# Modulation sums in pairs behind chosen VectorE operations, an earlier one-row Fourier split, and seven raw weight slots

## The chip, the core and the metric

The kernel runs on one core of a Trainium2 chip. The metric is the device time of one execution in microseconds (us). Three executions of the kernel before were timed, and one more was profiled. Its engines are named as the profile names them: PE (TensorE; PEld is its weight load), DVE (VectorE), ACT (ScalarE), POOL (GpSimd) and SP (SyncE, which here only issues DMAs).

## What is computed

One layer of a diffusion backbone over 1024 latent tokens of width 1024 and 256 context tokens. What matters here is the first part, from the modulation to the output projection; the expert part is 16 experts of a SwiGLU network over 128 tokens each.

```
mod = silu(c) @ w_mod + b_mod
sh1, sc1, g1, sh2, sc2, g2 = split(mod, 6)
hx = rmsnorm(x) * (1 + sc1) + sh1          # and the context with its own rows
u_f, u_x, u_g = split(hx @ w_in)           # 512 columns each
y_f = fft2(u_f, 4 groups of 128).real
xc  = conv4(u_x)                           # 4 channel tiles of 128 in the kernel
r, i = sigmoid(xc @ wa + ba), sigmoid(xc @ wi + bi)     # two directions
a   = exp(-8 r softplus(-lam));  h_t = a h_(t-1) + sqrt(1 - a^2) (i xc)
y_r = (h_forward + h_backward) * gelu(u_g)
x   = x + g1 * (concat(y_f, y_r) @ w_out)
hx2 = rmsnorm(x) * (1 + sc2) + sh2
out = rmsnorm(x + g2 * experts(hx2))
```

## The kernel before

All products are made of three matmuls with fp32r operands: `split` (lines 226 to 232) writes a tensor's upper part on ACT (line 227) and the rest on DVE (line 228, `raw - hi`), and `mm3` (line 608) issues hi by hi, hi by rest and rest by hi (line 611). So no product can end before DVE has made the rest of its weights: these tiles are called `wl` for the input projection, `gl` for the gates, `wol` for the output projection, `xcl` for the convolved tokens, `abl` and the one-row `xl` for the Fourier part.

The part before the experts runs in three stages. `phase_a` loads, normalizes and projects the first two channel tiles. `phase_c` goes through the four channel tiles t of the recurrent group: `conv(t)` (line 649), `lru_front(t)` with the gate products `g` and the sigmoids, exponentials and square roots on ACT, `lru_back(t)` (line 808) with `lru_scan` (line 711: two products and one scan of 1280 elements for each direction) on DVE, and `gelu(t)` for its gate; in between it makes the Fourier projections `uf` (`fourier_a`, line 876) and sends results to DRAM. `phase_f` makes the rest of the Fourier part group by group (`fb_dft`, `fb_split`, `fb_trig` with the products `pq`, `fb_evac` with the tiles `T` and `yf`), splits the output weights and makes the output projection `mx`, 8 token tiles long. After it come the router and the experts.

Four rows of the modulation (g1, sc2, sh2, g2) are not made on PE: `mod_acc(r, h)` (line 826) sums eight 128x512 pieces of w_mod, each times a column of `cond`, on DVE into an accumulator `macc`. The pieces come two by two, 512 KB a load, into two `mraw` slots, from POOL's DMA queue; the finished accumulator goes to DRAM (`accd`). There are 8 such calls, so 64 DVE instructions in 32 pairs. `mod_row` (line 842) reads the accumulators back in `phase_f` and adds the bias row on DVE (line 850).

The order of the instructions on each engine is made by a scheduler from the written order, priorities and when it holds an instruction ready; `high_priority` raises instructions, `pin` keeps one in the written order. In the kernel before, the calls of `mod_acc` stand in `phase_c` from line 741 on, without `pin`. Raw weights go through 3 slots of 128x512 (`wraw`), loaded from SP's queue; the next load into a slot is issued once the slot's split is done.

Of the kernel before, what the change touches and what calls it, by code (L numbers as in the profile page):

```python
# [9 lines left out]
F32 = mybir.dt.float32  # L10
F32R = mybir.dt.float32r
# [3 lines left out]
ALU = mybir.AluOpType  # L15

D = 1024
N = 1024
NCTX = 256
# [142 lines left out]
class Kern:  # L162
# [72 lines left out]
    def prologue(self, stop=None):  # L235
        tc, nc, a = self.tc, self.nc, self.a
        self.lg = self.cst.tile([128, 8, E], F32, name="lg")
        self.NC4, self.NP1 = 19, 4
        self.pr = self.sr.enter_context(tc.tile_pool(name="pr", bufs=1, side="right"))
        self.pro = self.sl.enter_context(tc.tile_pool(name="pro", bufs=1, side="left"))  # L240
        for tag, n, w, dt in (("wraw", 3, 512, F32), ("mraw", 2, 1024, F32), ("whi", 5, 512, F32R),
                              ("wlo", 5, 512, F32R)):
            self.pro.tile([128, w], dt, tag=tag, name=f"z_{tag}", bufs=n)
        for tag in ("xc", "xs"):
            self.c5(f"z_{tag}", tag=tag)
        self.c4("z_c4")
# [37 lines left out]
    def phase_a(self):  # L284
# [12 lines left out]

        def prefetch(ct, h, ht=False):
            t = self.pr.tile([128, 4, 128], F32, tag="ht", name=f"wr{ct}_{h}", bufs=2) if ht else self.pro.tile(
                [128, 4, 128], F32, tag="wraw", name=f"wr{ct}_{h}", bufs=3)  # L300
            nc.sync.dma_start(t.rearrange("p k c -> p (k c)"), a["win"][ct, h])
            self.wraw[ct, h] = t

# [345 lines left out]
    def conv(self, t):  # L649
        nc = self.nc  # L650
        u = self.u.pop(t)
        xc = self.c5(f"xc{t}", tag="xc")
        col = lambda i: self.cols[:, COL["cw"] + 4 * i + t:COL["cw"] + 4 * i + t + 1]
        cb = self.cols[:, COL["cb"] + t:COL["cb"] + t + 1]
        for o, n, q in ((0, N, NCTX), (N, NCTX, 0)):
            nc.scalar.activation(xc[:, q:q + n], u[:, o:o + n], AF.Identity, scale=col(1), bias=cb)
            for i, a, b in ((0, 1, n), (2, 0, n - 1), (3, 0, n - 2)):
                nc.vector.scalar_tensor_tensor(xc[:, q + a:q + b], u[:, o + a + i - 1:o + b + i - 1], col(i),
                                               xc[:, q + a:q + b], op0=ALU.mult, op1=ALU.add)
        self.xc[t] = xc  # L660

    def xsplit(self, t):
# [2 lines left out]
        self.xs[t] = h, l  # L665

    def load_gate(self, t):
        w = self.pro.tile([128, 4, 128], F32, tag="wraw", name=f"gr{t}", bufs=3)
        self.nc.sync.dma_start(w.rearrange("p k c -> p (k c)"), self.a["wgate"][t])
        self.graw[t] = w  # L670

# [38 lines left out]

    def lru_scan(self, d, r, g, a):
        V = self.nc.vector
        V.scalar_tensor_tensor(r, a, 1.0, r, op0=ALU.add, op1=ALU.mult)
        V.tensor_tensor(r, r, g, op=ALU.mult)  # L714
        s = slice(None) if d == 0 else slice(None, None, -1)
        V.tensor_tensor_scan(g[:, s], a[:, s], r[:, s], 0.0, op0=ALU.mult, op1=ALU.add)  # L716

    def phase_c(self, stop=None):
        nc = self.nc
        self.xc, self.xs, self.graw, self.gw = {}, {}, {}, {}  # L720
        self.ysp = self.dram.tile([7, 128, N], F32, name="ysp")
        self.yl = {}
        self.accd = self.dram.tile([4, 2, 128, 512], F32, name="accd")
        st = {}
        self.load_gate(0)
        self.conv(0)
        self.xsplit(0)
        self.load_trig()
        self.ux(2)
        self.gate_w(0)  # L730
        self.get(7)
        st[0] = self.lru_front(0)
        self.load_gate(1)
        self.conv(1)
        self.xsplit(1)
        self.ux(3)
        self.get(0)
        self.gate_w(1)
        self.lru_back(0, *st[0])
        self.fourier_a(0)  # L740
        self.mod_acc(0, 0)
        self.conv(2)
        self.get(8)
        self.load_gate(2)
        st[1] = self.lru_front(1)
        self.mod_acc(0, 1)
        self.xsplit(2)
        self.gelu(0)
        self.mod_acc(1, 0)
# [5 lines left out]
        self.mod_acc(1, 1)  # L755
        self.get(9)
        self.load_gate(3)
        st[2] = self.lru_front(2)
        self.mod_acc(2, 0)
        self.xsplit(3)  # L760
        self.gelu(1)
        self.mod_acc(2, 1)
        self.gate_w(3)
        self.get(2)
        self.lru_back(2, *st[2])
        self.fourier_a(2)
        self.mod_acc(3, 0)
        self.get(3)
        st[3] = self.lru_front(3)
        self.fourier_a(3)  # L770
        self.get(10)
        self.lru_back(3, *st[3])
        self.gelu(2)
        self.get(11)
        self.fd = {}
        self.fb_dft(0)
        self.fb_split(0)
        self.gelu(3)
        self.mod_acc(3, 1)
# [28 lines left out]
    def lru_back(self, t, st, a):  # L808
        nc = self.nc
        for d in range(2):  # L810
            self.lru_scan(d, *st[d], a[d])
        g0, g1 = st[0][1], st[1][1]
        nc.vector.tensor_tensor(g0[:, NCTX:], g0[:, NCTX:], g1[:, 0:N], op=ALU.add)
        self.yl[t] = g0[:, NCTX:]

    def gelu(self, t):
# [5 lines left out]
        nc.vector.tensor_tensor(gg, gg, self.yl.pop(t), op=ALU.mult)  # L822
        self.dump(f"yr{t}", gg)
        nc.sync.dma_start(self.ysp[3 + t], gg)

    def mod_acc(self, r, h):
        nc, a = self.nc, self.a
        m, s = (2, 4, 3, 5)[r], slice(512 * h, 512 * h + 512)
        acc = self.pr.tile([128, 512], F32, tag="ht", name=f"macc{m}{h}", bufs=2)
        for kp in range(KD // 2):  # L830
            w = self.pro.tile([128, 2, 512], F32, tag="mraw", name=f"mraw{m}{h}{kp}", bufs=2)
            nc.gpsimd.dma_start(w, a["wmod"][m, 2 * kp:2 * kp + 2, :, s].rearrange("k p c -> p k c"))
            for i in range(2):
                k = 2 * kp + i
                c = self.cond[:, k:k + 1]
                if k == 0:
                    nc.vector.tensor_scalar(acc, w[:, i], c, None, op0=ALU.mult)
                else:
                    nc.vector.scalar_tensor_tensor(acc, w[:, i], c, acc, op0=ALU.mult, op1=ALU.add)  # L839
        nc.gpsimd.dma_start(self.accd[r, h], acc)  # L840

    def mod_row(self, r, acc, b, ones, p):
        nc = self.nc
# [32 lines left out]
    def fourier_a(self, g):  # L876
# [8 lines left out]
        V.tensor_tensor(U[:, 0, 1:], p[:, 1:512], rev, op=ALU.add)  # L885
        V.tensor_tensor(U[:, 1, 1:], p[:, 1:512], rev, op=ALU.subtract)
# [19 lines left out]
    def fb_split(self, g):  # L906
# [68 lines left out]
    def phase_f(self):  # L975
# [7 lines left out]
        raws = {}  # L983

        def wo_raw(k, h, tag):
            raw = self.pro.tile([128, 512], F32, tag=tag, name=f"wor{k}{h}", bufs=3 if tag == "wraw" else 5)
            nc.sync.dma_start(raw, a["wout"][k][:, 512 * h:512 * h + 512])
            raws[k, h] = raw

# [28 lines left out]

        def half(n, p=128):
            tag = "wraw" if "s2" in n and n != "brows21" and "sh2" not in n else "wlo"  # L1020
            return self.pro.tile([p, 512], F32, tag=tag, name=n, bufs=3 if tag == "wraw" else 5)

        def row(r, name):
            p = self.p3(f"rowp{name}")
# [804 lines left out]
```

## Time and profile before

| | |
|---|---|
| timed executions | 1966.42, 1969.73, 1971.72 us; median 1969.73 |
| profiled execution, its own time | 1968.55 us |
| span of the profiled execution | 1966.7 us |
| PE busy | 1883.7 us, 96% of the span |
| DVE busy | 1749.7 us, 89% |
| ACT busy | 1357.4 us, 69% |
| mean granted TensorE clock | 0.985 |

The span runs from the first to the last instruction; the profiled execution's own time is 1.85 us longer and 1.2 us under the median of the three. An engine's busy time adds up over stages with different limits, so the table alone doesn't say which engine ends what; the rows further down are taken stage by stage.

### The profile page before, as it was taken

Reading aid. Unit: us, or ns where it says so; the run is one execution under the profiler, and the core shown is the slowest. Engines: PE = TensorE matmul, PEld = TensorE weight load, DVE = VectorE, ACT = ScalarE, POOL = GpSimd, SP = SyncE. Lnnn points to the kernel's source line nnn. Section 1 sums busy time; section 2 is a strip of 40 time slices with the busy share of each in tenths; the row PEclk is TensorE's granted clock in tenths of the full one; section 3 lists DMA queues with packets and bytes.
Section 4 is the critical chain, followed back from the end, with each engine's and each line's share of the span. In section 5 each row is a group of like instructions: output and inputs, shape, how many; then the busy total and the mean of one; then the engine's idle time right before and its main releaser. Section 6 shows DMA issues by size and latency. Waiting matters only on the chain.

```text
span 1966.7 us, 23514 instructions
## 1 busy us (share of the span) xinstructions
PE 1883.7 (96%) x8944; PEld 1530.9 (78%) x8944; DVE 1749.7 (89%) x1626; ACT 1357.4 (69%) x1094; POOL 126.6 (6%) x126
## 2 busy tenths in 40 slices
PE   7989879969999999999999999999999999999996
PEld 2777767857788888888888888888888888888884
DVE  7889787789999989899999999998989898989987
ACT  6568643346677777777777777777777777777775
POOL 2311100220000000000000000000000000000000
PEclk9999989979999999999999999999999999999998
DMA  8443554578999999999999999999999999999994
GB/s 333 126 148 123 193 174 150 200 279 332 352 352 388 383 376 390 370 395 371 391 362 395 359 409 370 387 364 397 372 384 380 391 379 373 390 383 390 371 391 172
DMA packets 113952, 651.27 MB, mean 331 GB/s; under 512 B 12743, under 2 KB 20472, under 8 KB 46254
## 3 DMA queue, kind: packets, MB, share of 16 engines
q1 hardware_dynamic: 100718, 602.55, 79.6%
q0 software_dynamic: 10816, 38.82, 7.0%
q10 hardware_dynamic: 2304, 8.39, 1.1%
q8 instruction: 70, 1.15, 0.2%
q14 instruction: 44, 0.36, 0.0%
HBM read 622.98 MB, written 26.74 MB: 330 GB/s over the span
## 4 chain that ended last, share of the span: by engine, by line
PE 79%; DVE 8%; DMA 6%; issue 5%; ACT 1%; POOL 0%; SPq 0%; POOLq 0%; DVEq 0%; ACTq 0%
PE gu L611 46%; PE y L611 23%; PE mx L611 4%; DMA mraw<-in_wmod_dram 3%; DVE lo L228 3%; PE ht L1620 2%; DMA wm<-in_wmod_dram 1%; DVE macc L839 1%; PE xt L1492 1%; DMA trr<-in_trig_dram 1%; PE hp L1185 1%; PE pq L611 1%; ACT hi L227 1%; DVE g L716 0%; DVE r L714 0%
## 5 line engine op out<-in xcount | busy, mean ns | idle before, releaser
L228 DVE TENSOR_TENSOR lo<-raw,hi 128x2048 fp32r<-128x2048 f32 x525 | 1196.9, 2295 | 120.6 <-ACT hi L227 119.7
L227 ACT ACTIVATE hi<-raw 128x2048 fp32r<-128x2048 f32 x525 | 1007.0, 1918 | 303.2 <-PE gu L611 204.4
L611 PE MATMUL gu<-hi,xgh 128*128 128x512 f32 x1408 | 556.2, 395 | 0.0
L611 PE MATMUL gu<-lo,xgh 128*128 128x512 f32 x1408 | 548.7, 390 | 1.4 <-DVE lo L228 1.4
L611 PE MATMUL gu<-hi,xgl 128*128 128x512 f32 x1408 | 548.9, 390 | 0.0
L611 PEld LDWEIGHTS gu<-hi,xgl 128*128 128x128 f32 x1408 | 264.4, 188 | 56.4 <-DVE xgl L228 0.2
L611 PEld LDWEIGHTS gu<-lo,xgh 128*128 128x128 f32 x1408 | 264.8, 188 | 55.7 <-DVE lo L228 1.8
L611 PEld LDWEIGHTS gu<-hi,xgh 128*128 128x128 f32 x1408 | 264.6, 188 | 52.7 <-issue 0.2
L611 PE MATMUL y<-hi,hh 128*128 128x512 f32 x704 | 282.0, 401 | 0.0
L611 PE MATMUL y<-hi,hl 128*128 128x512 f32 x704 | 275.9, 392 | 1.3 <-DVE hl L228 1.3
L611 PE MATMUL y<-lo,hh 128*128 128x512 f32 x704 | 274.8, 390 | 0.0
L611 PEld LDWEIGHTS y<-hi,hl 128*128 128x128 f32 x704 | 132.4, 188 | 30.4 <-DVE hl L228 1.8
L611 PEld LDWEIGHTS y<-lo,hh 128*128 128x128 f32 x704 | 132.9, 189 | 25.9 <-issue 0.2
L611 PEld LDWEIGHTS y<-hi,hh 128*128 128x128 f32 x704 | 132.7, 189 | 25.3 <-issue 0.2
L1613 ACT ACTIVATE hid<-gu 128x512 f32<-128x512 f32 x96 | 54.0, 563 | 82.4 <-PE gu L611 82.4
L1630 POOL DMA_INDIRECT accx<-ys,idx x15 | 23.9, 1590 | 1002.8 <-DVE ys L1629 929.7
L228 DVE TENSOR_TENSOR hl<-ht,hh 128x512 fp32r<-128x512 f32 x96 | 61.3, 638 | 0.0
L1614 DVE TENSOR_TENSOR hid<-hid,gu 128x512 f32<-128x512 f32 x96 | 61.0, 635 | 0.0
L839 DVE SCALAR_TENSOR_TENSOR macc<-mraw,cond,macc 128x512 f32<-128x512 f32 x56 | 41.8, 747 | 20.4 <-DMA mraw<-in_wmod_dram 19.5
L1620 PE MATMUL ht<-k_ident,hid 128*128 128x128 f32 x352 | 54.2, 272 | 3.0 <-DVE hid L1614 3.0
L1620 PEld LDWEIGHTS ht<-k_ident,hid 128*128 128x128 f32 x352 | 43.8, 140 | 16.5 <-DVE hid L1614 4.5
L227 ACT ACTIVATE hh<-ht 128x512 fp32r<-128x512 f32 x96 | 52.0, 541 | 1.5 <-PE ht L1620 1.5
(430 smaller groups left out, 1791.4 us busy)
## 6 DMA issues: line engine op xcount, KB each, us to landing
raw<-in_wg_dram SPq DMA_DIRECT2D x160, 1024.0 KB, 7.1
raw<-in_wu_dram SPq DMA_DIRECT2D x160, 1024.0 KB, 7.5
raw<-in_wd_dram SPq DMA_DIRECT2D x160, 1024.0 KB, 7.6
raw<-in_wt_dram SPq DMA_DIRECT2D x32, 1024.0 KB, 7.8
mraw<-in_wmod_dram POOLq DMA_DIRECT2D x32, 512.0 KB, 4.7
raw<-in_wdt_dram SPq DMA_DIRECT2D x16, 1024.0 KB, 6.9
wm<-in_wmod_dram SPq DMA_DIRECT2D x16, 512.0 KB, 9.8
wr<-in_win_dram SPq DMA_DIRECT2D x24, 256.0 KB, 3.6
```

What stands on the lines that cost most here:

```text
L227: i = self.nc.scalar.activation(hi, src, AF.Copy)
L228: j = (eng or self.nc.vector).tensor_tensor(lo, src, hi, op=ALU.subtract)
L611: i = nc.tensor.matmul(out, l, r, start=st, stop=sp)
L839: nc.vector.scalar_tensor_tensor(acc, w[:, i], c, acc, op0=ALU.mult, op1=ALU.add)
L1185: self.pin(nc.tensor.matmul(q[:, 1024:1024 + E], hT[:, k], wr[:, k], start=k == 0, stop=k == KD - 1))
L1492: nc.tensor.transpose(p[:, 128 * i:128 * i + 128], xg[:, 128 * k:128 * k + 128], self.ident)
L1613: nc.scalar.activation(hid[:, 0:w], p[:, 0, 0:w], AF.Silu)
L1614: nc.vector.tensor_tensor(hid[:, 0:w], hid[:, 0:w], up, op=ALU.mult)
L1620: self.nc.tensor.transpose(q[:, c:c + 128], hid[:, c:c + 128], self.ident)
L1630: self.nc.gpsimd.indirect_dma_start(out=self.accx, out_offset=bass.IndirectOffsetOnAxis(ap=idx[:, :1], axis=0), in_=ys, in_offset=None, co ...
```

## The change

`mod_acc` becomes a generator, `mod_gen`, which yields after each pair of DVE instructions and issues the load of the next pair ahead of the pair it works on. Its loads, sums and stores are all pinned to the written order. A counter, `tick`, moves it on: chosen DVE instructions (the convolution, the two products and the scan of `lru_scan`, the sum of the two directions, the gate product, the Fourier sums) report a cost, and each time the reported costs pass 1.7 one pair is emitted behind the instruction. The counter is switched on just ahead of `lru_back(0)`; what is left of the 32 pairs is emitted after `gelu(3)`. In `fb_split` the one-row split comes ahead of the two large ones and is raised twice. The raw weight slots go from 3 to 7, and the memory for them comes from the scratch of the dynamic DMAs, 8192 bytes instead of the default.

```
-        for tag, n, w, dt in (("wraw", 3, 512, F32), ("mraw", 2, 1024, F32), ("whi", 5, 512, F32R),
+        for tag, n, w, dt in (("wraw", 7, 512, F32), ("mraw", 2, 1024, F32), ("whi", 5, 512, F32R),
...
-        V.scalar_tensor_tensor(r, a, 1.0, r, op0=ALU.add, op1=ALU.mult)
-        V.tensor_tensor(r, r, g, op=ALU.mult)
+        self.tick(V.scalar_tensor_tensor(r, a, 1.0, r, op0=ALU.add, op1=ALU.mult), 1.5)
+        self.tick(V.tensor_tensor(r, r, g, op=ALU.mult), 1.5)
         s = slice(None) if d == 0 else slice(None, None, -1)
-        V.tensor_tensor_scan(g[:, s], a[:, s], r[:, s], 0.0, op0=ALU.mult, op1=ALU.add)
+        self.tick(V.tensor_tensor_scan(g[:, s], a[:, s], r[:, s], 0.0, op0=ALU.mult, op1=ALU.add), 2.8)
...
+        self.mg, self.cost = self.mod_gen(), None
...
+        self.cost = 0.0
         self.lru_back(0, *st[0])
         self.fourier_a(0)
-        self.mod_acc(0, 0)
...
         self.gelu(3)
-        self.mod_acc(3, 1)
+        for _ in self.mg:
+            pass
...
+    STEP = 1.7
+
+    def tick(self, i, cost):
+        if self.cost is None:
+            return
+        self.cost += cost
+        while self.cost >= self.STEP:
+            self.cost -= self.STEP
+            next(self.mg, None)
+
+    def mod_gen(self):
...
+        load(0)
+        for n, (r, h, kp) in enumerate(todo):
+            load(n + 1)
...
+                    self.pin(nc.vector.scalar_tensor_tensor(acc, w[n][:, i], c, acc, op0=ALU.mult, op1=ALU.add))
...
+            yield
...
         with self.tc.high_priority(offset=self.HP):
+            with self.tc.high_priority(offset=self.HP):
+                self.split(px[0:1, 0:128], xh, xl)
             for s in range(2):
...
-            self.split(px[0:1, 0:128], xh, xl)
...
-    nc = _bacc.Bacc("TRN2", target_bir_lowering=False, num_devices=1)
+    nc = _bacc.Bacc("TRN2", target_bir_lowering=False, num_devices=1, dynamic_dma_scratch_size=8192)
```

Three places show what this makes of DVE's order. The number behind a tile's name is the buffer's; a scan is printed as SCALAR_TENSOR_TENSOR, too (line 716 before, 717 now).

The first place is DVE ahead of the first scans, where `xcl1` splits the second channel tile and `g01` is a gate product of the first; `macc` is the accumulator of the sums and `r00` the first operand of `lru_back(0)`. Before:

```order
L839 SCALAR_TENSOR_TENSOR macc21_1294<-mraw213_1307,cond_185,macc21_1294 128x512 x2
L837 TENSOR_SCALAR macc40_1369<-mraw400_1370,cond_185 128x512
L839 SCALAR_TENSOR_TENSOR macc40_1369<-mraw400_1370,cond_185,macc40_1369 128x512
L228 TENSOR_TENSOR xcl1_1034<-xc1_1024,xch1_1033 128x1280
L699 TENSOR_TENSOR g01_1009<-g01_1009,xc0_822 128x1024
L700 TENSOR_TENSOR g01_1009<-g01_1009,xc0_822 128x256
L839 SCALAR_TENSOR_TENSOR macc40_1369<-mraw401_1374,cond_185,macc40_1369 128x512 x2
L839 SCALAR_TENSOR_TENSOR macc40_1369<-mraw402_1378,cond_185,macc40_1369 128x512 x2
L839 SCALAR_TENSOR_TENSOR macc40_1369<-mraw403_1382,cond_185,macc40_1369 128x512 x2
L837 TENSOR_SCALAR macc41_1475<-mraw410_1476,cond_185 128x512
L839 SCALAR_TENSOR_TENSOR macc41_1475<-mraw410_1476,cond_185,macc41_1475 128x512
L713 SCALAR_TENSOR_TENSOR r00_983<-a00_1014,r00_983 128x1280
```

And now:

```order
L228 TENSOR_TENSOR wl0_1_1124<-wr0_1_1117,wh0_1_1123 128x512
L698 TENSOR_TENSOR g00_984<-g00_984,xc0_822 128x1280
L228 TENSOR_TENSOR xcl1_1034<-xc1_1024,xch1_1033 128x1280
L700 TENSOR_TENSOR g01_1009<-g01_1009,xc0_822 128x1024
L701 TENSOR_TENSOR g01_1009<-g01_1009,xc0_822 128x256
L714 SCALAR_TENSOR_TENSOR r00_983<-a00_1014,r00_983 128x1280
```

In all, 26 of the 64 sums stood ahead of `r00` on DVE, and none does now.

The second place is DVE in `lru_back(0)`; `wl8_0` and `wl8_1` are the rests of the weights that PE's next projection `ug` reads. Before:

```order
L714 TENSOR_TENSOR r00_983<-r00_983,g00_984 128x1280
L714 TENSOR_TENSOR r01_1008<-r01_1008,g01_1009 128x1280
L716 SCALAR_TENSOR_TENSOR g00_984<-a00_1014,r00_983 128x1280
L716 SCALAR_TENSOR_TENSOR g01_1009<-a01_1017,r01_1008 128x1280
L228 TENSOR_TENSOR wl8_0_1226<-wr8_0_1221,wh8_0_1225 128x512
L813 TENSOR_TENSOR g00_984<-g00_984,g01_1009 128x1024
L228 TENSOR_TENSOR wl8_1_1230<-wr8_1_1223,wh8_1_1229 128x512
```

And now:

```order
L717 SCALAR_TENSOR_TENSOR g00_984<-a00_1014,r00_983 128x1280
L856 SCALAR_TENSOR_TENSOR macc00_1137<-mraw200_1133,cond_185,macc00_1137 128x512
L715 TENSOR_TENSOR r01_1008<-r01_1008,g01_1009 128x1280
L856 SCALAR_TENSOR_TENSOR macc00_1137<-mraw201_1135,cond_185,macc00_1137 128x512
L717 SCALAR_TENSOR_TENSOR g01_1009<-a01_1017,r01_1008 128x1280
L856 SCALAR_TENSOR_TENSOR macc00_1137<-mraw201_1135,cond_185,macc00_1137 128x512
L810 TENSOR_TENSOR g00_984<-g00_984,g01_1009 128x1024
L856 SCALAR_TENSOR_TENSOR macc00_1137<-mraw202_1141,cond_185,macc00_1137 128x512
L228 TENSOR_TENSOR wl8_0_1259<-wr8_0_1254,wh8_0_1258 128x512
L856 SCALAR_TENSOR_TENSOR macc00_1137<-mraw202_1141,cond_185,macc00_1137 128x512
L228 TENSOR_TENSOR wl8_1_1263<-wr8_1_1256,wh8_1_1262 128x512
L856 SCALAR_TENSOR_TENSOR macc00_1137<-mraw203_1145,cond_185,macc00_1137 128x512
```

The sums of the pairs `mraw200` to `mraw203` now stand one by one between the scans and the splits.

The third place is DVE where the second Fourier group is split; `abl1` and `xl1` are its large and one-row splits, `T20` the evacuation of the first group's `pq0`, and `accg11` and `accs21` are bias additions of `mod_row`. Before:

```order
L813 TENSOR_TENSOR g30_1789<-g30_1789,g31_1814 128x1024
L228 TENSOR_TENSOR abl1_2134<-ab1_2089,abh1_2133 128x512
L822 TENSOR_TENSOR gg3_2037<-gg3_2037,g30_1789 128x1024
L947 TENSOR_TENSOR T20_2144<-pq0_2106,T10_2143 128x256
L948 TENSOR_TENSOR T20_2144<-pq0_2106,T10_2143 128x256
L949 TENSOR_TENSOR T20_2144<-pq0_2106,T10_2143 128x256
L228 TENSOR_TENSOR xl1_2136<-abx1_2098,xh1_2135 1x128
L950 TENSOR_TENSOR T20_2144<-T10_2143,pq0_2106 128x256
```

And now:

```order
L228 TENSOR_TENSOR wol6_2189<-wor61_2083,woh6_2188 128x512
L870 TENSOR_TENSOR accg11_2455<-accg11_2455,browg11_2457 1x512
L870 TENSOR_TENSOR accs21_2500<-accs21_2500,brows21_2502 1x512
L819 TENSOR_TENSOR gg3_2055<-gg3_2055,g30_1807 128x1024
L228 TENSOR_TENSOR xl1_2136<-abx1_2098,xh1_2135 1x128
L228 TENSOR_TENSOR abl1_2134<-ab1_2089,abh1_2133 128x512 x2
L968 TENSOR_TENSOR T20_2144<-pq0_2106,T10_2143 128x256
L969 TENSOR_TENSOR T20_2144<-pq0_2106,T10_2143 128x256
```

`xl1` has gone ahead of `abl1` and of the first `T20` rows, and two `wol6` splits and four bias additions, which stood behind these, now stand ahead of them.

## Rows read from the trace of the kernel before

**Rows 1.** The page's chain that ended last, share of the span by engine.

```profile
PE 79%; DVE 8%; DMA 6%; issue 5%; ACT 1%; POOL 0%; SPq 0%; POOLq 0%; DVEq 0%; ACTq 0%
```

**Rows 2.** Stretches: us, then each engine's busy us (instructions), TensorE clock, DMA.

```profile
core 0: us, PE busy (x) PEld busy (x) DVE busy (x) ACT busy (x) POOL busy (x), PEclk, DMA share, GB/s
85.60:134.30 48.70, 48.37 (x239) 40.27 (x239) 38.09 (x48) 28.60 (x32) 10.21 (x15) 1.00 0.59 177
128.70:268.80 140.10, 116.33 (x537) 93.93 (x535) 122.31 (x144) 90.39 (x92) 15.56 (x23) 0.95 0.46 149
...
268.90:282.00 13.10, 12.27 (x71) 11.14 (x71) 10.13 (x27) 3.79 (x9) 0.00 (x0) 0.76 0.68 231
282.00:400.00 118.00, 117.66 (x629) 95.11 (x628) 91.33 (x263) 42.83 (x77) 17.81 (x10) 1.00 0.49 172
```

**Rows 3.** What PE waited for from 134.3 to 283: us, times, longest.

```profile
PE ug L611 <- DVE wl L228: 8.6, 2, 6.8
PE abx L903 <- DVE xl L228: 6.4, 1, 6.4
PE uf L611 <- DVE wl L228: 5.4, 1, 5.4
```

**Rows 4.** DVE's sums from 80 to 130: busy, mean ns, idle before, its releaser.

```profile
L839 DVE SCALAR_TENSOR_TENSOR macc<-mraw,cond,macc 128x512 f32<-128x512 f32 x22 | 16.5, 751 | 7.2 <-DMA mraw<-in_wmod_dram 6.7
L837 DVE TENSOR_SCALAR macc<-mraw,cond 128x512 f32<-128x512 f32 x4 | 2.5, 622 | 3.4 <-DMA mraw<-in_wmod_dram 3.4
```

**Rows 5.** Timeline of ACT: start, us, instruction, the square roots of the first tile.

```profile
123.17 2.44 ACT L805 ACTIVATE r<-r 128x1280 f32<-128x1280 f32 x2
```

**Rows 6.** Timeline of DVE: start, us, instruction.

```profile
128.70 2.89 DVE L713 SCALAR_TENSOR_TENSOR r<-a,r 128x1280 f32<-128x1280 f32 x2
...
168.13 0.49 DVE L837 TENSOR_SCALAR macc<-mraw,cond 128x512 f32<-128x512 f32 x1
...
182.49 1.21 DVE L813 TENSOR_TENSOR g<-g,g 128x1024 f32<-128x1024 f32 x1
...
185.75 0.74 DVE L839 SCALAR_TENSOR_TENSOR macc<-mraw,cond,macc 128x512 f32<-128x512 f32 x1
186.41 0.68 DVE L228 TENSOR_TENSOR gl<-gr,gh 128x512 fp32r<-128x512 f32 x1
187.01 0.74 DVE L839 SCALAR_TENSOR_TENSOR macc<-mraw,cond,macc 128x512 f32<-128x512 f32 x1
...
268.62 0.14 DVE L952 TENSOR_TENSOR yf<-pq,T 128x1 f32<-128x1 f32 x1
...
272.83 1.27 DVE L850 TENSOR_TENSOR accg<-accg,browg 1x512 f32<-1x512 f32 x2
```

**Rows 7.** What DVE waited for from 128.7 to 268.8: us, times, longest.

```profile
DVE macc L839 <- DMA mraw<-in_wmod_dram: 12.8, 6, 4.2
DVE macc L837 <- DMA mraw<-in_wmod_dram: 2.4, 2, 1.3
```

**Rows 8.** Loads of the sums: the page's issue row (us to landing), DVE and POOL timelines.

```profile
mraw<-in_wmod_dram POOLq DMA_DIRECT2D x32, 512.0 KB, 4.7
...
81.02 0.75 DVE L839 SCALAR_TENSOR_TENSOR macc<-mraw,cond,macc 128x512 f32<-128x512 f32 x1
...
82.08 0.70 POOL L832 DMA_DIRECT2D mraw<-in_wmod_dram  x1 [7.06 <-DVE macc L839]
...
196.32 1.41 POOL L832 DMA_DIRECT2D mraw<-in_wmod_dram  x2
...
201.87 1.54 DVE L839 SCALAR_TENSOR_TENSOR macc<-mraw,cond,macc 128x512 f32<-128x512 f32 x2 [4.01 <-DMA mraw<-in_wmod_dram]
```

**Rows 9.** Timeline of PE in the Fourier part: start, us, instruction, idle before.

```profile
268.90 0.77 PE L611 MATMUL pq<-trig,abh 128*128 128x258 f32 x2
...
275.20 2.08 PE L900 MATMUL ab<-dft,U 128*128 128x128 f32 x16
...
278.42 0.48 PE L611 MATMUL pq<-trig,abh 128*128 128x258 f32 x2 [0.83 <-DVE yf L952]
```

**Rows 10.** Timeline of POOL at the context's load: start, us, instruction, idle before.

```profile
45.81 1.27 POOL L228 TENSOR_TENSOR hTl<-ht,hTh 128x512 fp32r<-128x512 f32 x1 [1.88 <-ACT hTh L227]
```

More of the change, by code (lines that the diff above doesn't have):

```diff
@@ L299, in prefetch @@
             t = self.pr.tile([128, 4, 128], F32, tag="ht", name=f"wr{ct}_{h}", bufs=2) if ht else self.pro.tile(
-                [128, 4, 128], F32, tag="wraw", name=f"wr{ct}_{h}", bufs=3)
+                [128, 4, 128], F32, tag="wraw", name=f"wr{ct}_{h}", bufs=7)
             nc.sync.dma_start(t.rearrange("p k c -> p (k c)"), a["win"][ct, h])
@@ L657, in conv @@
             for i, a, b in ((0, 1, n), (2, 0, n - 1), (3, 0, n - 2)):
-                nc.vector.scalar_tensor_tensor(xc[:, q + a:q + b], u[:, o + a + i - 1:o + b + i - 1], col(i),
-                                               xc[:, q + a:q + b], op0=ALU.mult, op1=ALU.add)
+                self.tick(nc.vector.scalar_tensor_tensor(xc[:, q + a:q + b], u[:, o + a + i - 1:o + b + i - 1],
+                                                         col(i), xc[:, q + a:q + b], op0=ALU.mult, op1=ALU.add),
+                          1.3 if n == N else 0.5)
         self.xc[t] = xc
@@ L667, in load_gate @@
     def load_gate(self, t):
-        w = self.pro.tile([128, 4, 128], F32, tag="wraw", name=f"gr{t}", bufs=3)
+        w = self.pro.tile([128, 4, 128], F32, tag="wraw", name=f"gr{t}", bufs=7)
         self.nc.sync.dma_start(w.rearrange("p k c -> p (k c)"), self.a["wgate"][t])
@@ L745, in phase_c @@
         st[1] = self.lru_front(1)
-        self.mod_acc(0, 1)
         self.xsplit(2)
         self.gelu(0)
-        self.mod_acc(1, 0)
         self.gate_w(2)
@@ L754, in phase_c @@
         self.fourier_a(1)
-        self.mod_acc(1, 1)
         self.get(9)
@@ L758, in phase_c @@
         st[2] = self.lru_front(2)
-        self.mod_acc(2, 0)
         self.xsplit(3)
         self.gelu(1)
-        self.mod_acc(2, 1)
         self.gate_w(3)
@@ L766, in phase_c @@
         self.fourier_a(2)
-        self.mod_acc(3, 0)
         self.get(3)
@@ L812, in lru_back @@
         g0, g1 = st[0][1], st[1][1]
-        nc.vector.tensor_tensor(g0[:, NCTX:], g0[:, NCTX:], g1[:, 0:N], op=ALU.add)
+        self.tick(nc.vector.tensor_tensor(g0[:, NCTX:], g0[:, NCTX:], g1[:, 0:N], op=ALU.add), 1.2)
         self.yl[t] = g0[:, NCTX:]
@@ L821, in gelu, with load @@
         nc.scalar.activation(gg, p, AF.Gelu_apprx_tanh)
-        nc.vector.tensor_tensor(gg, gg, self.yl.pop(t), op=ALU.mult)
+        self.tick(nc.vector.tensor_tensor(gg, gg, self.yl.pop(t), op=ALU.mult), 1.2)
         self.dump(f"yr{t}", gg)
         nc.sync.dma_start(self.ysp[3 + t], gg)
-    def mod_acc(self, r, h):
-        nc, a = self.nc, self.a
[L828 to L832, printed above, removed]
+    STEP = 1.7
[7 more added lines that the diff above has]
+    def mod_gen(self):
+        nc, a = self.nc, self.a
+        todo = [(r, h, kp) for r in range(4) for h in range(2) for kp in range(KD // 2)]
+        w, acc = {}, {}
+        def load(n):
+            if n < len(todo):
+                r, h, kp = todo[n]
+                m, s = (2, 4, 3, 5)[r], slice(512 * h, 512 * h + 512)
+                w[n] = self.pro.tile([128, 2, 512], F32, tag="mraw", name=f"mraw{m}{h}{kp}", bufs=2)
+                self.pin(nc.gpsimd.dma_start(w[n], a["wmod"][m, 2 * kp:2 * kp + 2, :, s].rearrange("k p c -> p k c")))
+        load(0)
+        for n, (r, h, kp) in enumerate(todo):
+            load(n + 1)
+            if kp == 0:
+                acc = self.pr.tile([128, 512], F32, tag="ht", name=f"macc{r}{h}", bufs=2)
             for i in range(2):
@@ L836, in mod_acc @@
                 if k == 0:
-                    nc.vector.tensor_scalar(acc, w[:, i], c, None, op0=ALU.mult)
+                    self.pin(nc.vector.tensor_scalar(acc, w[n][:, i], c, None, op0=ALU.mult))
                 else:
-                    nc.vector.scalar_tensor_tensor(acc, w[:, i], c, acc, op0=ALU.mult, op1=ALU.add)
-        nc.gpsimd.dma_start(self.accd[r, h], acc)
+                    self.pin(nc.vector.scalar_tensor_tensor(acc, w[n][:, i], c, acc, op0=ALU.mult, op1=ALU.add))
+            del w[n]
+            if kp == KD // 2 - 1:
+                self.pin(nc.gpsimd.dma_start(self.accd[r, h], acc))
+            yield
     def mod_row(self, r, acc, b, ones, p):
@@ L884, in fourier_a @@
         rev = uT[:, 0:511]
-        V.tensor_tensor(U[:, 0, 1:], p[:, 1:512], rev, op=ALU.add)
-        V.tensor_tensor(U[:, 1, 1:], p[:, 1:512], rev, op=ALU.subtract)
+        self.tick(V.tensor_tensor(U[:, 0, 1:], p[:, 1:512], rev, op=ALU.add), 0.7)
+        self.tick(V.tensor_tensor(U[:, 1, 1:], p[:, 1:512], rev, op=ALU.subtract), 0.7)
         V.tensor_copy(U[:, 0, 0:1], p[:, 0:1])
@@ L985, in wo_raw @@
         def wo_raw(k, h, tag):
-            raw = self.pro.tile([128, 512], F32, tag=tag, name=f"wor{k}{h}", bufs=3 if tag == "wraw" else 5)
+            raw = self.pro.tile([128, 512], F32, tag=tag, name=f"wor{k}{h}", bufs=7 if tag == "wraw" else 5)
             nc.sync.dma_start(raw, a["wout"][k][:, 512 * h:512 * h + 512])
@@ L1020, in half @@
             tag = "wraw" if "s2" in n and n != "brows21" and "sh2" not in n else "wlo"
-            return self.pro.tile([p, 512], F32, tag=tag, name=n, bufs=3 if tag == "wraw" else 5)
+            return self.pro.tile([p, 512], F32, tag=tag, name=n, bufs=7 if tag == "wraw" else 5)
         def row(r, name):
```

## The prediction

> **What bounds the kernel now.** I read the chain that ended last first: 79% of it is PE and only 8% DVE [rows 1], so an edit on DVE matters only where PE waits for DVE. The table by stretches says where that is. From 85.6 to 134.3 PE is busy 48.37 of 48.70 us; from 282 to 400 it is busy 117.66 of 118.00; between them lie the recurrent part, in which PE is busy 116.33 of 140.10 us while DVE is busy 122.31, and the 13.1 us of the Fourier part with PE's clock at 0.76 [rows 2]. So the case is decided between 128.7 and 282.
>
> There the waits of PE come next: 8.6 us before `ug`, 6.4 before `abx`, 5.4 before `uf`, each ended by a split on DVE, none by a load of weights [rows 3]. DVE is the late engine. DVE's own waits say what DVE lacks: of its 17.8 us without work (140.10 less 122.31), 12.8 and 2.4 end with the landing of a piece of w_mod [rows 7], and 2.6 with anything else. So DVE ends this stretch, at the row at 268.62 that takes 0.14 and frees the product tile `pq0` [rows 6]; PE's next product starts at 268.90 [rows 9]. From there a chain from PE over ACT to DVE leads to the output projection at 282, and behind that PE is full, so I carry any shift at 268.8 to the end unchanged.
>
> **The change: taking the sums out of the early stretch.** 26 sums, 22 of one form and 4 of the other, and with them 6.7 + 3.4 = 10.1 us of waits for their loads, lie between 80 and 130 [rows 4]. The second order listing shows the 26 gone from ahead of `r00`. On PE this gains nothing, since PE was full there [rows 2]. On DVE it gains only until the next limit: `r00` needs the square roots of the first tile on ACT. The first of the two, started together at 123.17 and 2.44 us for both, ends at about 123.17 + 1.22 = 124.4 [rows 5]. ACT is fed by PE, which was full, so it comes no earlier. `r00` then starts near 124.5 in place of 128.70 [rows 6]: 4.2 us won, and DVE idles before it.
>
> **The change: the same sums later.** The 26 now stand in the stretch in which DVE is the late engine. From starts that follow one another on DVE, a sum takes 186.41 - 185.75 = 0.66 and a 128x512 split 187.01 - 186.41 = 0.60; a first product of an accumulator takes 0.49 [rows 6]. That is 22 x 0.66 = 14.5 and 4 x 0.49 = 2.0. By the last pair of order listings two `wol6` splits (2 x 0.60 = 1.2) and four bias additions (1.27 for two [rows 6], less the overlap of neighbours 0.60 each, 2.4) come ahead of the row that frees `pq0`, too. DVE's work from `r00` to that row grows from 122.3 to 122.3 + 14.5 + 2.0 + 1.2 + 2.4 = 142.4. Starting at 124.5, with no wait at all, it would end at 266.9, 1.9 before today's 268.8.
>
> **The change: the load waits.** So all hangs on how long DVE will stand without work, 17.8 before. There are two slots, so a load starts when the pair before last is done, and must land while DVE does everything else up to the pair after next. The turn of a slot is 0.3 from the end of a pair (81.02 + 0.75 = 81.77) to POOL's next issue at 82.08, and 4.7 from issue to landing, the median of 32 [rows 8]: 5.0. Before, long runs of sums stood back to back and paid it every time; now other work stands between. How much, the order and the rows' durations tell. An example from the second listing: between the last sum of `mraw201` and the first of `mraw203` stand an addition of 1.2 (the 1.21 at 182.49 [rows 6]), two sums of `mraw202` at 0.66 and two splits at 0.60, together 3.7. The load needs 5.0, so DVE stands 1.3. Added up in this way over all pairs, the work between is 3.7 to 7.6, 4.9 in the mean; 15 of the 30 gaps are under 5.0, and their shortfalls come to 10 us (waits that one gap pays are not paid again by the next). It is steep: nothing if a slot turned in under 3.7, 20 at 5.8. For the upper end a row stands: two loads issued together at 196.32 ended DVE's wait at 201.87, 5.5 later [rows 8], and 5.5 + 0.3 = 5.8. I take the median, 10. The 2.6 of other waits I keep: the sums now delay the splits that PE needs, as in the second listing `wl8_0`, but the same splits start 4.2 earlier. DVE then frees `pq0` at 266.9 + 10 + 2.6 = 279.5: 10.7 later.
>
> The Trainium skill would price the load otherwise: "DMA: Bandwidth & Descriptors", section "Anatomy of one DMA — SWDGE (gpsimd) path", gives 2.0 us plus the bytes over 436 GB/s, which for 512 KB I estimate at 3.2. The 4.7 of this trace speaks against it for loads amid this kernel's other traffic; by the page the sum would come without load waits (266.9 + 2.6, a gain of less than 1 us).
>
> **The change: the small edits.** The one-row split ahead of the large ones aims at the 6.4 us of `abx` [rows 3]. The third listing shows it ahead of the first evacuation of `pq0`; but PE's next product needs `pq0` free as well, so the last of that evacuation still decides. Bound of a gain: `pq` products take 268.90 to 275.20 = 6.3 in one group, and from 275.20 on PE runs again without that gap [rows 9]. At a clock of 0.76 [rows 2] the 13.1 us would be 13.1 x 0.24 = 3.1 shorter at the upper clock, if all of it were PE's own time; a PE that rested less before could get back that much. With DVE still late PE rests as long, so: zero. Seven raw weight slots: no wait of PE ended with such a load [rows 3], so zero. On SP one weight load is now issued ahead of the context's loads; POOL has 1.88 us of idle time at that place [rows 10], more than such an issue costs: zero. Half of the DMA scratch: POOL has two of these loads outstanding at most, so zero, with the bound below. After 282 nothing is moved.
>
> **The rivals.** First, *slower by the load waits*, as summed up: 10.7 later at `pq0`, 1968.55 + 10.7 = 1979.3. For it speaks that PE's waits and DVE's shortage lie in the same stretch; the spread from 4 us of waits (+4.7) to 20 (+20.7) gives 1973 to 1989.
>
> Second, *every load lands in time*: with less bunching on the queues a slot turns in under 3.7, the load waits go, and DVE ends at 266.9 to 269.5, 1.9 before to 0.7 after today: 1966.7 to 1969.3, no change. Against it stands the median of 4.7; for it, that DVE waits for ACT or PE in some of these gaps, which fills them for nothing. It decides where all load waits stay under 17.8 - 10 = about 4 us together (4 + 2.6 + 266.9 = 273.5 would be +4.7, still within the measurement). The fit of the Trainium skill quoted above would make this the outcome.
>
> Third, *faster*: on top of the second, the early one-row split keeps PE at work, and the 3.1 of slow clock come back: -1.9 - 3.1 = -5.0, 1963.6. It is faster than the kernel before by a measurable amount only if another 0.9 go, for which the splits would have to release PE earlier, too.
>
> Fourth, *POOL's queue gets slower by the change*: if half the scratch held one such load at a time, a load would be issued only when the last had landed, 32 x 5.0 = 160 us for a stretch of 142.4 of work. That is 18 beyond the work, and DVE would end at 266.9 + 18 + 2.6 = 287.5, +18.7: 1987 and more. Seven loads of raw weights in a burst beside them would act in the same direction. Nothing in the trace speaks for either.
>
> **How the numbers follow.** First case 0.72, second 0.15, third 0.06, fourth 0.07. The forecast is 1979 us; the median of the runs lies 1.2 above the profiled execution, which I leave to the range. The range goes from 1967, the best of the second case, to 1990, the 20 us end of the first. About 0.3%, 5.9 us, is what a measurement of this kernel can tell from no change: slower by more 0.79 (first and fourth; the first's end under it is set against the second's end over it), within it 0.15, faster 0.06.
>
> **What the changed profile would show.** No sum before about 124 and DVE idle ahead of `r00`, which starts near 124.5, if the first step is right; earlier, if ACT gained from a free DVE. DVE's waits for w_mod between there and the row that frees `pq0` should be 4 to 20 us, about 10, in pieces of 0.2 to 1.5 after short gaps, and the median landing still near 4.7; under 4 us of landing makes the second case. That row should end near 279.5, and the first `mx` product come near 293 in place of 282. PE should still wait for splits on DVE before `ug`, `uf` and `abx`, in sum for longer, and for no load of weights. The length from the first `mx` product to the end should be the same. I am wrong if DVE is not late in this stretch any more, if PE's waits go away although DVE has more to do, or if the time differs after 282.

## The result, and the profile after

Four executions of the changed kernel took 1982.6 to 1983.9 us, median 1983.1; the kernel before took 1970.6 beside them. The ratio is 1.0065, with a 95% interval from 1.0053 to 1.0077: slower by 12.5 us. The forecast was 1979, slower, with a range from 1967 to 1990. Both hold. The span of the profiled execution is 1980.8 against 1966.7, 14.1 more. The way there differs from the prediction at two steps, and two errors of opposite sign partly cancel.

The stretches of the changed kernel (columns as in [rows 2]) begin with DVE's first recurrence, end with the row that frees `pq0`, and go on to the first and the last `mx` product:

```profile
core 0: us, PE busy (x) PEld busy (x) DVE busy (x) ACT busy (x) POOL busy (x), PEclk, DMA share, GB/s
124.10:286.80 162.70, 132.09 (x555) 105.38 (x554) 141.96 (x175) 94.22 (x98) 25.86 (x38) 0.88 0.54 173
...
286.80:298.60 11.80, 10.90 (x70) 9.99 (x71) 8.11 (x23) 3.43 (x8) 0.00 (x0) 0.86 0.55 176
298.60:406.50 107.90, 107.51 (x556) 86.44 (x555) 81.59 (x225) 40.18 (x69) 16.42 (x10) 1.00 0.47 156
```

DVE's work between the same two marks went from 122.3 to 141.96, its time without work from 17.8 to 20.7. The Fourier chain behind it took 11.8 in place of 13.1, at a clock of 0.86 in place of 0.76; the projection is as long as before.

What DVE waited for in that stretch (us, times, longest; the second row is the idle time just ahead of the first recurrence), to set beside [rows 7]:

```profile
DVE macc L856 <- DMA mraw<-in_wmod_dram: 13.6, 10, 2.7
DVE r L714 <- ACT r L802: 7.3, 1, 7.3
DVE macc L854 <- DMA mraw<-in_wmod_dram: 6.3, 5, 2.9
DVE abl L228 <- ACT abh L227: 0.7, 1, 0.7
```

13.6 + 6.3 = 19.9 us in 15 waits for pieces of w_mod; before it was 15.2 in 8. PE's waits from 85 to 300, beside [rows 3]:

```profile
PE ug L611 <- DVE wl L228: 7.9, 2, 4.1
PE ug L611 <- ACT gg L818: 7.9, 2, 5.1
PE g L611 <- ACT r L694: 6.0, 3, 2.9
PE uf L611 <- DVE wl L228: 3.8, 2, 3.4
PE pq L611 <- DVE yf L973: 2.2, 2, 1.4
PE ug L611 <- DVE U L908: 2.2, 1, 2.2
...
```

The 6.4 before `abx` is gone, and the waits for splits before `ug` and `uf` came to 11.7, where the three were 20.4. Waits for ACT (7.9 and 6.0) have come in. ACT in turn waited 20.5 us for DVE in the stretch, 17.5 before; that this is what makes it late is likely, but no single row shows it. PE was also busy for longer, 132.09 us in place of 116.33, partly for 18 more products, partly at a granted clock of 0.88 in place of 0.95. PE's clock is not what made the stretch longer: DVE was at work or waiting for a load in 141.96 + 19.9 of its 162.70 us. Two rows of DVE's timeline mark the ends of the stretch, beside [rows 6]:

```profile
124.07 2.89 DVE L714 SCALAR_TENSOR_TENSOR r<-a,r 128x1280 f32<-128x1280 f32 x2 [7.28 <-ACT r L802]
...
286.63 0.15 DVE L973 TENSOR_TENSOR yf<-pq,T 128x1 f32<-128x1 f32 x1
```

### The profile page after: what moved, and what is told of

It reads as the page before. It is cut to its first block, busy times and chain, and to the rows that moved or that the text cites. A ratio compares the mean times of both kernels' runs of the same rounds, so it can differ in the third digit from the quotient of the medians.

```text
span 1980.8 us, 23517 instructions
## 1 busy us (share of the span) xinstructions
PE 1895.9 (96%) x8944; PEld 1539.6 (78%) x8944; DVE 1748.5 (88%) x1626; ACT 1357.4 (69%) x1093; POOL 128.9 (7%) x126
## 4 chain that ended last, share of the span: by engine, by line
PE 78%; DVE 5%; issue 1%; ACT 1%; DMA 1%; POOLq 0%; DVEq 0%; ACTq 0%
PE gu L611 46%; PE y L611 23%; PE mx L611 4%; DVE lo L228 2%; PE ht L1641 2%; PE xt L1513 1%; PE hp L1206 1%; ACT hi L227 1%; PE pq L611 1%; DMA xg<-hxd,idx 0%; PE hp L1197 0%; ACT junkf L1686 0%; DMA raw<-in_wg_dram 0%; PE mx7a L611 0%; PE mx7b L611 0%
## 5 line engine op out<-in xcount | busy, mean ns | idle before, releaser
L611 PEld LDWEIGHTS y<-hi,hl 128*128 128x128 f32 x704 | 132.4, 188 | 30.4 <-DVE hl L228 1.8
L856 DVE SCALAR_TENSOR_TENSOR macc<-mraw,cond,macc 128x512 f32<-128x512 f32 x56 | 41.7, 745 | 13.6 <-DMA mraw<-in_wmod_dram 13.6
```

The lines of the kernel that those rows point to most:

```text
L611: i = nc.tensor.matmul(out, l, r, start=st, stop=sp)
L856: self.pin(nc.vector.scalar_tensor_tensor(acc, w[n][:, i], c, acc, op0=ALU.mult, op1=ALU.add))
```

## The experiments

Times are medians; the change against the kernel before is from runs on the same chip. "Freed" is the start of the row that frees `pq0`, 268.62 before and 286.63 after. These times differ between profiles for a reason ahead of the stretch: the first `ux` product starts anywhere from 85.2 to 90.0 us. The kernel before has its first recurrence at 128.7, and three runs with its order of the sums have it at 132.1 to 133.0. So a single time is good to 4 or 5 us, and the length between the two columns says more.

| kernel | us | ratio, 95% interval | first recurrence | freed |
|---|---|---|---|---|
| changed kernel | 1983.1 | 1.0065 [1.0053, 1.0077] | 124.1 | 286.6 |
| sums only | 1983.8 | 1.0065 [1.0048, 1.0082] | 128.2 | 287.6 |
| slots and scratch only | 1968.4 | 0.9989 [0.9979, 0.9998] | 132.1 | 271.5 |
| one-row split only | 1969.9 | 1.0003 [0.9993, 1.0013] | 133.0 | 270.7 |
| changed, four w_mod slots | 1975.5 | 1.0029 [1.0017, 1.0040] | 125.8 | 280.6 |
| before, four w_mod slots | 1958.1 | 0.9935 [0.9918, 0.9952] | 133.0 | 262.2 |
| changed, counter on early | 1979.3 | 1.0043 [1.0026, 1.0060] | 133.9 | 289.5 |
| both of these on the changed | 1966.1 | 0.9975 [0.9965, 0.9986] | 127.4 | 274.2 |
| changed, 16 of 64 sums | 1946.4 | 0.9877 [0.9857, 0.9897] | 127.4 | 251.6 |
| changed, 12 pairs first | 1973.2 | 1.0013 [1.0003, 1.0024] | 130.3 | 282.7 |
| before, four slots, split first | 1959.4 | 0.9945 [0.9928, 0.9962] | 134.4 | 263.6 |
| before, five w_mod slots | 1954.7 | 0.9922 [0.9905, 0.9940] | 132.4 | 259.1 |
| scratch only | 1969.7 | 0.9992 [0.9982, 1.0001] | 132.1 | 273.9 |

**Which part of the change.** The first run keeps only the sums' move (the diff is against the changed kernel, with the four other uses of the slots changed alike):

```
-        for tag, n, w, dt in (("wraw", 7, 512, F32), ("mraw", 2, 1024, F32), ("whi", 5, 512, F32R),
+        for tag, n, w, dt in (("wraw", 3, 512, F32), ("mraw", 2, 1024, F32), ("whi", 5, 512, F32R),
...
-            with self.tc.high_priority(offset=self.HP):
-                self.split(px[0:1, 0:128], xh, xl)
...
+            self.split(px[0:1, 0:128], xh, xl)
...
-    nc = _bacc.Bacc("TRN2", target_bir_lowering=False, num_devices=1, dynamic_dma_scratch_size=8192)
+    nc = _bacc.Bacc("TRN2", target_bir_lowering=False, num_devices=1)
```

> The changed kernel with three raw weight slots, the default DMA scratch and the one-row split last, as before: only the moving of the sums is left of the change. My theory (the sums' move carries all of it: DVE's 20 us more of work in the recurrent part, less the 4.2 it starts earlier, plus load waits): 1983 us, 1979 to 1987, with DVE's waits for w_mod near 20 us as in the changed kernel, and the last 128x1 evacuation of the first Fourier group near 287. Rival (the bunch of raw loads or the smaller scratch slows the loads of w_mod): 1975 or less, with load waits near 10 us and fewer landings over 6 us.

Measured 1983.8, with 18.1 us of waits for w_mod. The sums' move is the whole loss. The second and the third run make the other parts alone on the kernel before, by the same lines the other way round.

> The kernel before with seven raw weight slots and half of the DMA scratch, and nothing else. My theory (no wait of PE ended with a weight load, so neither part does anything): 1968 to 1973. Rival (the larger bursts and the scratch slow the loads of w_mod): 1975 or more, with DVE's waits for w_mod well above the 25.4 us of before.

> The kernel before with the one-row split ahead of the two large ones, and nothing else. My theory (the product behind it needs the tile that the evacuation frees just after): PE's 6.4 us ahead of abx become about the same wait ahead of pq, 1967 to 1973. Rival (the wait for the one-row split is what keeps PE): the 6.4 us go and the kernel takes 1964 or less.

Neither loses: 1968.4 and 1969.9. With the slots and the scratch the kernel is even 2 us faster, by little more than the interval (more on this at the end). With the split first, PE's waits from 134 to 290 show the exchange that the prediction named:

```profile
PE pq L611 <- DVE yf L953: 5.3, 2, 4.4
...
PE abx L903 <- DVE xl L228: 2.0, 1, 2.0
```

The 6.4 before `abx` fell to 2.0, and PE waits 5.3 for the evacuation just behind it, where it had waited 0.8 [rows 9].

**Are the load waits the loss?** Four slots of w_mod in place of two, paid by the raw weight slots, and loads three pairs ahead:

```
-        for tag, n, w, dt in (("wraw", 7, 512, F32), ("mraw", 2, 1024, F32), ("whi", 5, 512, F32R),
+        for tag, n, w, dt in (("wraw", 3, 512, F32), ("mraw", 4, 1024, F32), ("whi", 5, 512, F32R),
...
-        load(0)
+        for n in range(3):
+            load(n)
...
-            load(n + 1)
+            load(n + 3)
...
```

> The changed kernel with four slots for w_mod in place of two and loads issued three pairs ahead; the memory comes from the raw weight slots, three as before, half scratch as in the changed kernel. Same order of the sums. My theory (20 us of DVE's time in the recurrent part are waits for two slots): DVE's waits for w_mod fall under 2 us, the first Fourier group is freed near 267 to 270 in place of 286.7, and the kernel takes 1983 - 17 = 1966, 1963 to 1970. Rival (the sums' place between the scans delays the splits and gate products, and the waits only show it): waits for w_mod fall, but others take their place, 1976 or more.

Measured 1975.5, between the two theories. The waits for w_mod fell as expected, but others came (DVE from 80 to 300):

```profile
DVE r L714 <- ACT r L802: 11.2, 3, 7.3
...
DVE macc L857 <- DMA mraw<-in_wmod_dram: 4.2, 3, 2.0
...
DVE wol L228 <- ACT woh L227: 1.6, 1, 1.6
DVE accg L871 <- DMA browg<-in_rows_dram: 1.6, 1, 1.6
```

15.7 us of load waits went (19.9 to 4.2); the time from the first recurrence to the freeing row fell by only 162.6 - 154.8 = 7.8 (280.6 - 125.8 = 154.8), and the kernel by 7.6. About half of the load waits stood where DVE now waits for ACT instead: 11.2 - 7.3 = 3.9 more before the recurrences, and smaller ones, in all 7.7 inside the stretch where it had been 0.7. PE in turn waited 8.2 us for one split ahead of `uf`, twice as long as in the changed kernel: the sums still stand ahead of that split. So my theory fell in its size. The same slots in the kernel before tell the rest:

```
-        for tag, n, w, dt in (("wraw", 3, 512, F32), ("mraw", 2, 1024, F32), ("whi", 5, 512, F32R),
+        for tag, n, w, dt in (("wraw", 3, 512, F32), ("mraw", 4, 1024, F32), ("whi", 5, 512, F32R),
...
-    nc = _bacc.Bacc("TRN2", target_bir_lowering=False, num_devices=1)
+    nc = _bacc.Bacc("TRN2", target_bir_lowering=False, num_devices=1, dynamic_dma_scratch_size=8192)
```

> The kernel before with four slots for w_mod in place of two (memory from half of the DMA scratch) and nothing else. First theory (DVE is the late engine and every wait for a load is lost): its 15.2 us of such waits in the recurrent part go and the kernel takes 1956 to 1960. Second theory, from the run with four slots in the changed kernel, where 16 us of waits less gave 8: about half of it, 1961 to 1966. Third (the waits only cover waits for ACT and PE): 1968 to 1972, the waits for ACT growing by as much.

Measured 1958.1, the first theory: 13.0 less than the kernel before beside it, and faster than both kernels. The scheduler, free to place the sums and with more of them loaded, put 37 ahead of the first recurrence where 26 stood; that started at 132.99, within the spread named above, and the stretch from there to the freeing row took 129.2 in place of 139.9. DVE's waits for w_mod from 80 to 290 fell to these two rows:

```profile
DVE macc L839 <- DMA mraw<-in_wmod_dram: 4.7, 4, 2.5
...
DVE macc L837 <- DMA mraw<-in_wmod_dram: 1.8, 3, 0.9
```

Not all of the 13.0 is load waits. DVE's work in the stretch fell from 122.3 to 117.8, because more sums stand ahead of it; its load waits there fell from 15.2 to 1.9, and its waits for ACT grew from 1.3 to 10.1. Some of it may also come from the halved scratch, which by itself took 0.9 off the median (last run).

The four runs make a table. With two slots the new order costs 1983.1 - 1970.6 = 12.5; with four, where waits for loads are small in both, 1975.5 - 1958.1 = 17.4. So the new order's loss does not go with the load waits: four slots help the order before at least as much (13.0, or some 11 if the scratch is set aside, against 1983.1 - 1975.5 = 7.6). That leaves the work that was moved, which the next runs test.

**The moved work, from the other side.** Three runs move sums back in the changed kernel, one leaves sums out. The counter on from the start of the stage:

```
-        self.mg, self.cost = self.mod_gen(), None
+        self.mg, self.cost = self.mod_gen(), 0.0
...
-        self.cost = 0.0
         self.lru_back(0, *st[0])
```

> The changed kernel with the counter switched on from the start of the second stage, so that some 11 of the 64 sums stand again ahead of the first recurrence, in DVE's idle time before 124 us, and the rest keep their spacing. My theory (the loss is the work that was moved into the stretch where DVE is late): 11 x 0.66 = 7 us less work there and the last of the load waits earlier, 1983 - 7 to 1983 - 12, 1971 to 1976. Rival (the loss is the spacing between scans, whatever their number): 1980 or more.

Measured 1979.3: 3.8 less than the changed kernel, half of the least that I expected. The 11 early sums were there, but three of them not early: pinned ahead of the recurrence, they made DVE wait for their load, and the recurrence started at 133.88.

```profile
131.05 0.49 DVE L853 TENSOR_SCALAR macc<-mraw,cond 128x512 f32<-128x512 f32 x1 [10.23 <-DMA mraw<-in_wmod_dram]
131.57 0.75 DVE L855 SCALAR_TENSOR_TENSOR macc<-mraw,cond,macc 128x512 f32<-128x512 f32 x1
133.21 0.75 DVE L855 SCALAR_TENSOR_TENSOR macc<-mraw,cond,macc 128x512 f32<-128x512 f32 x1 [0.89 <-DMA mraw<-in_wmod_dram]
133.88 1.49 DVE L714 SCALAR_TENSOR_TENSOR r<-a,r 128x1280 f32<-128x1280 f32 x1
```

POOL's timeline shows why that load was late. The eight pieces of the Fourier tables (`trr`) go through the same two slots, and with POOL's order fixed the next load of w_mod is issued only behind the last of them:

```profile
98.24 0.57 POOL L880 DMA_DIRECT2D trr<-in_trig_dram  x1 [4.89 <-DVE macc L855]
...
126.35 0.71 POOL L842 DMA_DIRECT2D mraw<-in_wmod_dram  x1
```

The recurrence started 9.8 later than in the changed kernel (133.9 against 124.1). Of this 3.6 stand already ahead of ACT's square roots (126.37 against 122.77), so the fixed order cost about 6; the kernel won in spite of it. With four slots as well, this wait is gone:

> The two before together: four slots, loads three pairs ahead, and the counter on from the start of the second stage. My theory (work moved back and load waits gone add up): 1975.5 - 7 = 1968, 1964 to 1971. If the load waits were only covering others: as the early counter alone.

Measured 1966.1, 9.4 less than with four slots alone, as the theory has it: 11 to 12 sums are 8 us of DVE's work.

Then 12 pairs emitted at once behind the first tile's split, so that 24 sums stand ahead of the recurrence, two slots:

```
         self.xsplit(0)
+        for _ in range(13):
+            next(self.mg)
         self.load_trig()
```

(The thirteenth pair is emitted there, too; the scheduler placed it behind the first two instructions of the recurrence.)

> The changed kernel with 12 of the 32 pairs emitted right behind the split of the first tile, so that 24 sums stand ahead of the first recurrence as 26 did before; the others stay in pairs behind the chosen operations, two slots. My theory (the loss is the 26 sums moved behind the first recurrence, not the pairs, the pins or the spacing): the loss goes, 1967 to 1973. Rival (the spacing between scans and its load waits cost, whatever stands early): 1978 or more.

Measured 1973.2: 10 of the 12.5 us are gone, just above the expectation. The 2.4 that are left (0.6 to 4.7 by the interval) are what pairs, pins and spacing cost together, or up to 5 if the end of the program is 2.6 shorter by the scratch (last run). In this lies one wait of 9.9 us that ends at 171, again for a load that stood behind the Fourier tables on POOL. The last one leaves 48 of the 64 sums out:

```
-            if n < len(todo):
+            if n < len(todo) and n % (KD // 2) == 0:
...
-                else:
+                elif kp == 0:
...
```

> The changed kernel with 16 of the 64 sums and a quarter of their loads (the other pieces of w_mod are left out of the modulation): the price of the sums in their place. My theory (DVE is late from the first recurrence to the Fourier part): 48 x 0.66 = 32 us of work and nearly all of the load waits go, until PE's own 116 us of work in that stretch or ACT limit: 1945 to 1960. Rival (ACT's and PE's chain from tile to tile limits, not DVE): 1966 or more.

Measured 1946.4: 36.7 us less than the changed kernel, for 48 x 0.66 = 31.7 us of work and 19.9 of load waits taken from DVE. So DVE is the late engine for most of these 51.6 us, and not for all: of the 124.3 us that the stretch still takes PE is busy 116.4.

**Going on from four slots.** The one-row split ahead of the others in that kernel, and a fifth slot from another half of the scratch (4096 bytes, `mraw` 5):

> The kernel before with four slots for w_mod and the one-row split first: whether that split gains once DVE is less late. PE waits 1.8 us for it in the run with four slots. Theory (the evacuation is right behind): 1957 to 1960, no gain. Rival: 1.8 us less, 1956.

> The kernel before with five slots for w_mod, paid by three quarters of the DMA scratch. 6.5 us of waits for w_mod are left with four. Theory: 1953 to 1958, if half of these go. Rival (a quarter of the scratch holds up POOL's loads, or more sums in front only move the first recurrence later): 1958 or more.

The split gives nothing, 1959.4. Five slots give 1954.7, 16 us less than the kernel before and the fastest with all of the work in it; DVE waits 1.6 us for loads in the stretch, so no wait shows the quarter of the scratch holding anything up.

## Why the prediction was right, and where it was off

**Sums out of the early stretch: right.** The first recurrence was to start at 124.5, with DVE idle ahead of it; it started at 124.07 after 7.28 us of waiting for ACT. PE gained nothing there.

**The same sums later: right.** DVE's work was to be 142.4; it was 141.96. That the 12.5 to 17.4 us of loss come in the main from it is what the table of four and the runs with sums moved back show.

**The load waits: the term that was mis-sized.** 15 gaps shorter than a slot's turn were counted, and 15 waits came; but they took 19.9 us, not 10. The step that failed took the median landing for all turns, where short turns save nothing and long ones cost in full. The median was as assumed:

```profile
mraw<-in_wmod_dram POOLq DMA_DIRECT2D x32, 512.0 KB, 4.6
```

Read off the POOL and DVE timelines for the 30 loads that wait for a slot, the turn from a pair's end to the next landing was 5.5 in the mean, and 6.0 to 7.6 in ten of them. Worked out with the spacing that the changed kernel's trace has, turns of 5.0 would give 9.8 us of waits in 15 places, as counted; stores kept ahead of the loads and every landing at 4.6 would give 12.9; the turns as they were give 19.9. So the late landings make some 7 of the missing 10, the stores some 3. Both causes show in one example, POOL and then DVE:

```profile
161.03 0.56 POOL L859 DMA_DIRECT2D accd<-macc  x1 [2.76 <-DVE macc L856]
161.58 0.71 POOL L843 DMA_DIRECT2D mraw<-in_wmod_dram  x1
```

```profile
159.98 0.75 DVE L856 SCALAR_TENSOR_TENSOR macc<-mraw,cond,macc 128x512 f32<-128x512 f32 x1
...
168.44 0.75 DVE L856 SCALAR_TENSOR_TENSOR macc<-mraw,cond,macc 128x512 f32<-128x512 f32 x1 [2.70 <-DMA mraw<-in_wmod_dram]
```

The pair ended at 160.73. At the end of each accumulator its store is issued ahead of the next load, which starts at 161.58 in place of 161.03; and that load took some 6.8 to land. Why some loads take half as long again is open: it happens in the kernel before, too, where the longest took 7.8. The upper end of the range, a turn of 5.8 and 20 us, had it in. By the Trainium skill ("DMA: Bandwidth & Descriptors", section "Anatomy of one DMA — SWDGE (gpsimd) path") this load was estimated at 3.2; the trace's 4.6 disagrees, and the second rival, which it spoke for, did not come. That rival's own bound was worked out wrongly: 17.8 - 10 is 7.8, not about 4. Nothing else hung on it, and 19.9 lies beyond both.

**Other waits: 2.6 were kept, 0.8 came** (20.7 less 19.9). The run with four slots shows the link: a load wait and a wait for ACT can cover the same time. Two signs came otherwise than they were named: PE's waits for splits were to be longer in sum and were shorter (11.7 against 20.4), with waits for ACT and a lower clock in their place, and the load waits were to be 0.2 to 1.5 long and went up to 2.9.

So the freeing row came 18.0 later, not 10.7. The difference of 7.3 is 9.9 from load waits, less 1.8 from others and 0.4 each from start and work.

**"Carried to the end unchanged": wrong by 4 us, in the other direction.** The shift was 18.0 at the freeing row and about 16.7 at the first and the last `mx` product: the chain between ran at the higher clock for longer and was 1.3 shorter, a gain that I had put at zero with a bound of 3.1. Then 2.6 more went in the last 8 us of the span, at POOL's last store. Half of the DMA scratch, costed at nothing, gives that back. That the 7.3 too much at the freeing row and these 4 too little at the end offset each other is luck: the span grew by 14.1 against the 10.7 of the sum, where at `pq0` it was 18.0. The timeline of POOL, before, after, and with the scratch alone:

```profile
core 0 of [0], span 1966.7 us
...
1959.18 0.97 POOL L1689 DMA_INDIRECT out_dram<-ysL,idx  x1 [77.67 <-DMA out_dram<-fin]
```

```profile
core 0 of [0], span 1980.8 us
...
1975.90 0.97 POOL L1710 DMA_INDIRECT out_dram<-ysL,idx  x1 [75.44 <-DMA out_dram<-fin]
```

```profile
core 0 of [0], span 1968.4 us
...
1963.46 0.97 POOL L1689 DMA_INDIRECT out_dram<-ysL,idx  x1 [75.43 <-DMA out_dram<-fin]
```

From this store to the end of the span it is 7.5, 4.9 and 4.9 us. The last of these differs from the kernel before by a single argument:

```
-    nc = _bacc.Bacc("TRN2", target_bir_lowering=False, num_devices=1)
+    nc = _bacc.Bacc("TRN2", target_bir_lowering=False, num_devices=1, dynamic_dma_scratch_size=8192)
```

> The kernel before with half of the DMA scratch (8192 bytes) and nothing else. In the traces so far the time from POOL's last store to the end of the span was 7.5 us in the three kernels with the default scratch and 4.6 to 4.9 in the nine with less. New theory (the program's end waits on POOL for a time that grows with the scratch): that tail is 4.9, everything ahead of it as before, and the kernel takes 2.6 us less, 1967.5 to 1969. Old step of the prediction (the scratch does nothing): the tail stays 7.5 and the time is that of the kernel before.

The tail is as the new theory has it, in every kernel with half of the scratch, and 7.5 or 7.6 in all three with the default. The time itself moved by 0.9, with an interval from 3.5 less to 0.2 more: 2.6 lies in it, and so does next to nothing. In this profile the stretch ahead ran 4 to 5 us later than in that of the kernel before, which is spread from run to run. So the shorter tail is shown, and its worth in the median is not settled beyond that interval; the run with slots and scratch points the same way (0.9989).

**Seven raw weight slots and the one-row split: right.** The split alone gave 1.0003; the slots gave 0.9989 together with the scratch, which alone gave 0.9992. **The fourth rival** (POOL held up by less scratch) did not come, even at a quarter.

## What to carry to other kernels

Before filler work is moved on an engine, read from the stretch it leaves and the stretch it enters which engine is late in each: an idle engine's slot ahead of a recurrence was worth 10 of the 12 us here, however neatly the work was spread later. For double buffering compare the work between two uses with the spread of the turns, not with their median, since only the long turns count; and where one more slot can be had, try that first. Four slots for the same loads were worth 11 to 13 us, with no line of the order changed by hand; the scheduler used them to place 11 more sums early. And where the order is fixed by hand, look at what else goes through the same slots: two runs here had a wait of 10 us behind the Fourier tables.

## What was not expected of the hardware

The time from the last indirect store on POOL to the end of the span depends on the size of the dynamic DMA scratch: 7.5 or 7.6 us with the default, 4.9 with 8192 bytes, 4.6 with 4096 (1953.1 - 1948.5). The store itself lands 3.3 us after its issue in all four kernels below, so the difference does not lie in the data. It lies in the last long instruction on POOL, a DRAIN that starts just ahead of the store's row. The third number behind the count is its length in ns; before, after, the scratch alone, and five slots with the quarter of the scratch:

```profile
L1825 POOLq DRAIN  x3: 46/102/7001, 1959.0 to 1966.5; - x3
...
L1846 POOLq DRAIN  x3: 46/103/4346, 1975.7 to 1980.5; - x3
...
L1825 POOLq DRAIN  x3: 46/103/4351, 1963.2 to 1968.1; - x3
...
L1825 POOLq DRAIN  x3: 46/102/3934, 1948.3 to 1952.8; - x3
```

What POOL does within it no row tells.
